# Hybrid Conformer/SSD block: sums of weight blocks by adding loads and another VectorE order at the hand-over to the feed forward

## The chip, the core and the metric

One core of a Trainium2 chip runs the whole block in one program. TensorE (PE in the profile) does the matmuls, VectorE (DVE) and ScalarE (ACT) the elementwise work, GpSimd (POOL) a few small operations and the loads that add to what lies in memory on the chip, SyncE (SP) issues most of the plain loads. The metric is the device time of one execution in microseconds (us). Before the change it is 1030.28 us, the median of three runs (1030.25 to 1030.38).

## What is computed

A block of a language model on 512 tokens of width 1024: a mixer with two branches (a gated convolution and a state space scan), then a gated feed forward. The mixer is unchanged here; what matters is its end and the feed forward behind it.

```python
h = rms_norm(x, mix_pre_g); proj = h @ w_in
...
mixed = (g_conv * conv_out + g_ssm * ssm_out) @ w_out
x = x + rms_norm(mixed, mix_post_g)
h = rms_norm(x, ffn_pre_g)
gt, up = jnp.split(h @ w_gate_up, 2, axis=-1)
f = (jax.nn.silu(gt) * up) @ w_down
x = x + rms_norm(f, ffn_post_g)
```

`FFN_HIDDEN` is 2816, so the gate and the up part have 22 tiles of 128 columns each, and `rms_norm(y, g)` is `y * rsqrt(mean(y*y) + 1e-6) * g`.

## The kernel before

**Arithmetic.** Every float32 operand of a matmul is split into a high and a low half of a shorter type, and a product takes three matmuls (`mm3`, L186 to L188: high by high, high by low, low by high). The high half is a cast by ScalarE, the low half the difference by VectorE (`halve`, L930 and L935). For the units listed in `ADD_LO`, ScalarE writes the negated high half instead (L932) and an adding load on GpSimd's queue adds the weight to it from memory (L933).

**The feed forward by Strassen-Winograd.** The product `h @ w_gate_up` is done in 22 pairs of tiles, the units `u = 0..21` (in pairs: the even units are gate parts, the odd ones up parts; pair `f = u // 2`), each with seven block products in place of eight. A unit has two weight blocks of 128 x 1024, each read as a left and a right half of 512 columns: (a11, a12) and (a21, a22). Weight sums of a unit are made by VectorE in `prep_s`: s1 = a21 + a22 (L956), s3 = a11 + a21 (L959, into a21's place), s2 = s1 + a11 (L960), s4 = s2 + a12 (L961). The activations' blocks b11, b21, b22 and their sums t1 to t4 are made in `transposed` once the four token tiles are there. TensorE multiplies a11 by b11, a12 by b21, s1 by t1, s2 by t2, s3 by t3, s4 by b22 and a22 by t4, 12 matmuls of 256 columns for each product. Products that belong together are added in one PSUM bank where that is possible, and by VectorE otherwise (`add`, L1107).

**The hand-over.** Token tile 3 is the last of the mixer. `tm_step` puts out its last product with the output weights (`tm_wo`; their last matmuls read the tiles named m1h and m1l in the pool `mp`). `residual(3)` then takes the mean square of each half (ScalarE, tile jk), the sum pm_a (VectorE, L873), the power -1/2 (GpSimd, rs_a, L874), the scaled sum with the old x (VectorE, xr, L1006), again mean square, pm_b, rs_b, and a diagonal matrix dg = identity times rs_b (VectorE, L1010). TensorE transposes xr by multiplying with dg (tile ptr, L1023). `transposed(3)` makes the tiles xg (L1030 on VectorE, L1035 on ScalarE) and from them t1 (L1061), t2 (L1062), t3 (L1068), t4 (L1070) and b22 with their halves. TensorE meanwhile runs the first products of units 0 to 2 (`first`), which need only the tokens of earlier tiles for the first part.

**Order.** Each engine runs its instructions in the order of its queue; a waiting instruction holds what stands behind it. The order is decided when the program is built, from the program's text, the tiles' dependences and a planner; `not_before(a, b)` keeps instruction a behind b. The list `hold` gives two instructions, for ScalarE and VectorE, behind which the halves of weights have to stay at that place. `start` (L1205) gives the order of the last products of the first four units: `v0 x0 v1 w0 y0`, then `x1 w1 z0 y1` and so on, where v is s1's product, x is s2's, w is s4's with b22, y is s3's and z is a22's with t4 - each letter a function (v1, x2, v2, x3, x4 in the code).

**Results of units.** Gate units write to tiles sg, up units to two slots each of f32, an array of 22 slots of 2 KB a partition. f32 is made (L1158) after `mix.close()`, so it takes space on the chip that the pool `mp` has given up; its first write has to wait for all that was there. For a unit, `begin` copies the first product out of PSUM (ScalarE, L1118) and adds the second (VectorE, L1107); `v1` copies s1's product from its own bank v (ScalarE, L1170), and the product with b22 later starts anew in that same bank (`v2`), so it waits for that copy.

**Loads.** `w_raw(n)` loads the n-th weight block (512 KB) on SP's queue into one of five buffers, in the order of `ORDER` (L148).

## Time and profile before

| | us |
|---|---|
| median of 3 runs | 1030.28 (1030.25 to 1030.38) |
| the profiled execution | 1036.17 |
| its span, first to last instruction | 1034.4 |
| TensorE busy | 1024.2 |
| VectorE busy | 814.3 |
| ScalarE busy | 609.0 |
| GpSimd busy | 96.4 |
| mean granted TensorE clock | 0.998 |

The profiled execution is longer than the runs that are only timed, so times of the trace are compared with the trace's own span, and times of runs with runs. Engines have the names given above; PEld is the loading of weights into TensorE's array. A timeline row has the start, the duration, the engine, the line of the kernel, the operation, output and inputs by the names of tiles, their size, and in brackets the idle time before it with what ended that. A tile's name stands there without its number: `xy` is a bank with two quarter results of a unit, `v` the bank of s1's product, `ptr` a transposed tile, `whi_g`/`wlo_g` and `chi_g`/`clo_g` the high and low halves of a weight block (two names for two places), `dhi`/`dlo` those of s1, `s` is s1, `raw` a weight block as loaded, `f` is f32. The hand-over lies between 690 and 745 us of the span.

### The profile page before, as it was taken

The page shows a single profiled execution, that of the slowest core. Times are in us where ns is not written, and L with a number is a line of the kernel's source. Part 1 is how long each engine was busy: PE and PEld are TensorE (multiplying, and loading weights), DVE is VectorE, ACT ScalarE, POOL GpSimd, SP SyncE. Part 2 cuts the span into 40 slices and gives each one's busy share as a digit, 9 for nine tenths or more (in the row PEclk, how much of TensorE's full clock was granted, in tenths as well). Part 3 has the DMA queues.
Part 4 walks back from the last instruction along what each step waited for, and adds up shares of the span by engine and source line. Part 5 has one row for each costly group of instructions (what it writes and reads, how often), then busy time and mean ns, then how long its engine had stood idle before and what let it go on. Part 6 is the DMA issues. An engine that isn't in the chain of part 4 may idle for free.

```text
span 1034.4 us, 15686 instructions
## 1 busy us (share of the span) xinstructions
PE 1024.2 (99%) x6089; PEld 890.9 (86%) x6089; DVE 814.3 (79%) x1184; ACT 609.0 (59%) x1032; POOL 96.4 (9%) x122
## 2 busy tenths in 40 slices
PE   9999999999999999999999999999999999999997
PEld 7898889888888888888888888889999999998885
DVE  7899976959594979398976455579997788799874
ACT  7655776575748464844532673366665565568552
POOL 0101101110111011101100000010000000001000
PEclk9999999999999999999999999999999999999999
DMA  8567634655546454644452223433565345469622
GB/s 298 156 164 213 165 81 140 184 157 148 135 131 163 124 157 128 163 122 122 110 133 84 82 85 99 183 105 121 167 184 157 105 143 146 123 197 278 214 82 82
DMA packets 42458, 150.82 MB, mean 146 GB/s; under 512 B 4880, under 2 KB 5904, under 8 KB 41360
## 3 DMA queue, kind: packets, MB, share of 16 engines
q1 hardware_dynamic: 30672, 104.66, 29.9%
q0 software_dynamic: 9504, 38.80, 19.0%
q10 hardware_dynamic: 2208, 6.36, 1.8%
q8 instruction: 48, 0.79, 0.3%
q14 instruction: 26, 0.21, 0.1%
HBM read 145.54 MB, written 4.26 MB: 145 GB/s over the span
## 4 chain that ended last, share of the span: by engine, by line
PE 93%; DVE 3%; ACT 2%; issue 1%; DMA 0%; POOL 0%; SPq 0%; ACTq 0%; POOLq 0%; DVEq 0%
PE xy L187 4%; PE xy L186 4%; PE xy L188 4%; PE pz L187 3%; PE pz L188 3%; PE pz L186 3%; PE pso L186 3%; PE pso L187 3%; PE pso L188 3%; PE px L188 3%; PE px L187 3%; PE px L186 3%; PE yv L187 2%; PE yv L188 2%; PE yv L186 2%; PE yd L636 2%
## 5 line engine op out<-in xcount | busy, mean ns | idle before, releaser
L152 ACT CAST whi<-raw 128x1024 fp32r<-128x1024 f32 (+2 forms) x116 | 115.0, 1003 | 157.3 <-PE pso L187 37.5
L444 DVE SCALAR_TENSOR_TENSOR a<-v,prm_t,a 128x511 f32<-128x511 f32 (+15 forms) x240 | 179.8, 752 | 16.1 <-ACT a L441 13.8
L158 DVE TENSOR_TENSOR wlo<-raw,whi 128x1024 fp32r<-128x1024 f32 (+2 forms) x76 | 85.8, 1134 | 42.8 <-ACT whi L152 42.1
L156 POOL DMA_DIRECT2D wlo<-in_w x40 | 35.7, 893 | 353.5 <-ACT wlo L155 120.9
L188 PE MATMUL pz<-whi,hlo 128*128 128x512 f32 (+2 forms) x160 | 56.3, 352 | 0.0
L187 PE MATMUL pz<-wlo,hhi 128*128 128x512 f32 (+2 forms) x160 | 56.1, 351 | 0.0
L186 PE MATMUL pz<-whi,hhi 128*128 128x512 f32 (+2 forms) x160 | 55.4, 353 | 0.0
L186 PE MATMUL px<-hhi,whi 128*128 128x512 f32 x128 | 50.2, 392 | 0.0
L186 PE MATMUL pso<-yh,whi 128*128 128x512 f32 x128 | 50.0, 393 | 0.0
L188 PE MATMUL px<-hhi,wlo 128*128 128x512 f32 x128 | 49.8, 389 | 0.0
L187 PE MATMUL px<-hlo,whi 128*128 128x512 f32 x128 | 49.8, 389 | 0.0
L187 PE MATMUL pso<-yl,whi 128*128 128x512 f32 x128 | 49.7, 390 | 0.0
L188 PE MATMUL pso<-yh,wlo 128*128 128x512 f32 x128 | 49.7, 389 | 0.0
L930 ACT CAST whi_g<-raw 128x1024 fp32r<-128x1024 f32 x40 | 41.3, 1053 | 13.7 <-PE yv L187 8.6
L528 DVE SCALAR_TENSOR_TENSOR x<-px,prm_t,x 128x511 f32<-128x511 f32 (+2 forms) x48 | 34.7, 741 | 13.8 <-ACT x L526 13.8
L935 DVE TENSOR_TENSOR wlo_g<-raw,whi_g 128x1024 fp32r<-128x1024 f32 x34 | 41.1, 1218 | 5.1 <-ACT whi_g L930 4.7
L155 ACT ACTIVATE wlo<-whi 128x1024 fp32r<-128x1024 f32 x40 | 42.2, 1055 | 0.3
L426 ACT ACTIVATE L<-L,nacs 128x128 f32<-128x128 f32 x128 | 38.8, 389 | 0.5 <-POOL L L419 0.4
L186 PEld LDWEIGHTS pz<-whi,hhi 128*128 128x128 f32 x160 | 30.2, 189 | 3.9
L187 PEld LDWEIGHTS pz<-wlo,hhi 128*128 128x128 f32 x160 | 30.2, 188 | 3.8
L188 PEld LDWEIGHTS pz<-whi,hlo 128*128 128x128 f32 x160 | 30.1, 188 | 3.7
L930 ACT CAST chi_g<-raw 128x1024 fp32r<-128x1024 f32 x24 | 24.8, 1050 | 11.4 <-PE yv L187 5.1
(656 smaller groups left out, 3344.8 us busy)
## 6 DMA issues: line engine op xcount, KB each, us to landing
raw<-in_w SPq DMA_DIRECT2D x186, 512.0 KB, 4.5
wlo<-in_w POOLq DMA_DIRECT2D x40, 512.0 KB, 6.8
L<-scr POOLq DMA_DIRECT2D x8, 1024.0 KB, 7.1
wlo_g<-in_w POOLq DMA_DIRECT2D x11, 512.0 KB, 7.1
clo_g<-in_w POOLq DMA_DIRECT2D x7, 512.0 KB, 5.3
xr<-in_x ACTq DMA_DIRECT2D x4, 512.0 KB, 4.7
x2d<-xr ACTq DMA_DIRECT2D x4, 512.0 KB, 2.9
xres<-x2d SPq DMA_DIRECT2D x4, 512.0 KB, 3.7
```

What stands on the lines that cost most here:

```text
L152: act.copy(hi[:, c], src[:, c])
L155: act.activation(lo[:, c], hi[:, c].bitcast(F32), AF.Copy, scale=-1.0)
L156: mark["lo"] = pool.dma_start(lo[:, c], w[n][:, c].bitcast(F32R), accum_op=ALU.add)
L158: mark["wlo"] = dve.tensor_tensor(out=lo[:, c], in0=src[:, c], in1=hi[:, c].bitcast(F32), op=ALU.subtract)
L186: mark["pe"] = pe.matmul(ps, lh, rh, start=start, stop=False, skip_group_check=more)
L187: pe.matmul(ps, lh, rl, start=False, stop=False, skip_group_check=more)
L188: mark["pe3"] = pe.matmul(ps, ll, rh, start=False, stop=stop, skip_group_check=more)
L426: act.activation(L[:, h, c, :], L[:, h, c, :], AF.Exp, bias=nacs[:, c, HG * g + h : HG * g + h + 1])
L444: return dve.scalar_tensor_tensor(out=va[j][:, d:], in0=vs[j][:, : T - d], scalar=col("dw_w", j * KC + KC - 1 - d), in1=va[j][:, d:], op0= ...
L528: dve.scalar_tensor_tensor(out=a[:, d:], in0=ps[:, : T - d], scalar=col("ssm_w", i * KS + KS - 1 - d), in1=a[:, d:], op0=ALU.mult, op1=ALU ...
L930: a_ = act.copy(hi, src)
L935: d_ = dve.tensor_tensor(out=lo, in0=src, in1=hi.bitcast(F32), op=ALU.subtract)
```

## The change

Nothing that is multiplied changes, and neither does TensorE's order of instructions.

- *Sums by loads.* For units 1 and 2, s1 is loaded as a21 (`load_s1`, a plain load on SP's queue) and a22 is added to it by an adding load on GpSimd's queue (`add_s1`); s3 is made by adding a11 to a21 in the loaded block in the same way (`add_s3`). s1 of unit 2 lies in the room of m1l, and the second blocks of units 1 and 2 (tile b12) in the room of m1h, so their loads are issued after the last `tm_wo` matmul that reads these. VectorE has L956 and L959 less for these two units.
- *Unit 4's low half* by ScalarE and an adding load (`ADD_LO`).
- *Order of VectorE around token tile 3.* `hold` is set after xr in place of after mg; in unit 0's halves the later part is held behind dg; unit 1's sum s2 is held in place of s1; the sum of unit 3 is held behind t4's low half. `add_s1` and `add_s3` are held behind the last power.
- *d1.* The first half of unit 1's result gets a tile of its own (d1, in the pool of sg) and `begin(1)` comes earlier. The second half takes its slot of f32 only at the copy in `v1`. The product with the gate is written to f32 by the last step (`f_out`), and the same function names the places of other units as before.

In the built order the instructions of VectorE are 5 fewer, ScalarE has one more, and GpSimd issues 5 more loads. On GpSimd's queue the add to s1 of unit 2 stands ahead of the power for rs_b of token tile 3; the adds to b12 stand behind it. On ScalarE's queue the copy of s1's product of unit 1 into f32 stands behind the two whi_g casts, the table load and the Silu of unit 0; in the kernel before it stood ahead of them.

```diff
--- before.py
+++ after.py
@@ -75,7 +75,7 @@
 EARLY_U = 4
 DMA_EVERY = 2
 DMA_FROM = 8
-ADD_LO = (2, 3) + tuple(range(7, FF // P, 2))
+ADD_LO = (2, 3, 4) + tuple(range(7, FF // P, 2))
 GU_AHEAD = 5
 MOV_AT = 192
 S_AHEAD = 5
@@ -136,12 +136,15 @@
 
 
     raws, split, more_raw = {}, {}, []
+    late = {}
     seq = {key: n for n, key in enumerate(ORDER)}
     GU = range(seq["gu", 0], seq["w1", 0])
 
     def w_raw(n):
-        if n < len(ORDER) and n not in raws:
-            if more_raw and n >= GU[0] and n % 7 < 2:
+        if n < len(ORDER) and n not in raws and late.get(n, True) is not None:
+            if n in late:
+                raws[n] = late[n]
+            elif more_raw and n >= GU[0] and n % 7 < 2:
                 raws[n] = more_raw[0].tile([P, 1024], F32, tag="raw2", bufs=2, name=f"raw{n}")
             else:
                 raws[n] = wp.tile([P, 1024], F32, tag="raw", bufs=RAW_BUFS, name=f"raw{n}")
@@ -871,7 +874,7 @@
         rs = sm.tile([P, 1], F32, tag="rs1", bufs=2, name=f"rs_{tag}")
         m = sm.tile([P, 1], F32, tag="pm1", bufs=2, name=f"pm_{tag}")
         mark["pm"] = dve.tensor_scalar(out=m, in0=ss[0], scalar1=ss[1], scalar2=RMS_EPS, op0=ALU.add, op1=ALU.add)
-        pool.tensor_tensor(out=rs, in0=m, in1=neg_half[:, :1], op=ALU.pow)
+        mark["pow"] = pool.tensor_tensor(out=rs, in0=m, in1=neg_half[:, :1], op=ALU.pow)
         return rs
 
     def scale_of(srcs, pool_, tag):
@@ -946,18 +949,41 @@
             again = w[seq[("gu", 2 * u)]] if u in ADD_LO else None
             halve(("a11", "a12"), u, g_raw(u, 0), room or pair_of_tiles(), again)
 
+    s1s = {}
+
+    def load_s1(u):
+
+        if u == 1:
+            s1s[u] = w2.tile([P, T], F32, tag="s1", bufs=2, name=f"s1_{u}")
+        else:
+            s1s[u] = mp.tile([P, T], F32, tag="m1l", name=f"s1_{u}")
+        nc.sync.dma_start(s1s[u], w[seq["gu", 2 * u + 1]][:, :T])
+
+    def add_s1(u):
+
+        return pool.dma_start(s1s[u], w[seq["gu", 2 * u + 1]][:, T:], accum_op=ALU.add)
+
+    def add_s3(u):
+
+        return pool.dma_start(g_raw(u, 1)[:, :T], w[seq["gu", 2 * u]][:, :T], accum_op=ALU.add)
+
     def prep_s(u):
 
         if u >= NF or (u, "s1") in forms:
             return
         ra, rb_ = g_raw(u, 0), g_raw(u, 1)
         (a11, a12), (a21, a22) = [(r[:, :T], r[:, T:]) for r in (ra, rb_)]
-        s1_ = w2.tile([P, T], F32, tag="s1", bufs=2, name=f"s1_{u}")
-        sum_ = dve.tensor_tensor(out=s1_, in0=a21, in1=a22, op=ALU.add)
+        if u in s1s:
+            s1_ = s1s[u]
+        else:
+            s1_ = w2.tile([P, T], F32, tag="s1", bufs=2, name=f"s1_{u}")
+            sum_ = dve.tensor_tensor(out=s1_, in0=a21, in1=a22, op=ALU.add)
+            if u == 3:
+                not_before(sum_, mark["t4"][1])
+            dve.tensor_tensor(out=a21, in0=a11, in1=a21, op=ALU.add)
+        sum_ = dve.tensor_tensor(out=a11, in0=s1_, in1=a11, op=ALU.add)
         if hold:
             not_before(sum_, hold[1])
-        dve.tensor_tensor(out=a21, in0=a11, in1=a21, op=ALU.add)
-        dve.tensor_tensor(out=a11, in0=s1_, in1=a11, op=ALU.add)
         dve.tensor_tensor(out=a12, in0=a11, in1=a12, op=ALU.add)
 
         def s1_halves():
@@ -967,6 +993,8 @@
             halve(("s2", "s4"), u, ra, pair_of_tiles())
             if u != 1:
                 s1_halves()
+            if u == 0:
+                hold[1] = mark["dg"]
             halve(("s3", "a22"), u, rb_, pair_of_tiles())
 
         if u == 1:
@@ -986,6 +1014,8 @@
             if k == 0 and mark.get("chain"):
                 not_before(m, last)
 
+    b12_raw = [seq["gu", 2 * u + 1] for u in (1, 2)]
+    late.update({n: None for n in b12_raw})
     xrs, xgs = {}, {}
 
     def residual(t, ps):
@@ -997,14 +1027,15 @@
         ss = []
         for n, c in enumerate(cols2):
             ss.append(mean_sq(ps[n], pbp, f"a{t}", n))
-            m = dve.tensor_tensor(out=mg[:, c], in0=ps[n], in1=gpost0[:, c], op=ALU.mult)
-        if t == 3:
-            hold += [mark["sq"], m]
+            dve.tensor_tensor(out=mg[:, c], in0=ps[n], in1=gpost0[:, c], op=ALU.mult)
+        first_sq = mark["sq"]
         rs = factor(ss, f"a{t}")
         ss = []
         for n, c in enumerate(cols2):
-            dve.scalar_tensor_tensor(out=xr[:, c], in0=mg[:, c], scalar=rs, in1=xr[:, c], op0=ALU.mult, op1=ALU.add)
+            m = dve.scalar_tensor_tensor(out=xr[:, c], in0=mg[:, c], scalar=rs, in1=xr[:, c], op0=ALU.mult, op1=ALU.add)
             ss.append(mean_sq(xr[:, c], pbp, f"b{t}", n))
+        if t == 3:
+            hold += [first_sq, m]
         rs = factor(ss, f"b{t}")
         dg = pbp.tile([P, P], F32, tag="dg", name=f"dg{t}")
         mark["dg"] = dve.tensor_scalar(out=dg, in0=ident, scalar1=rs, scalar2=None, op0=ALU.mult)
@@ -1094,6 +1125,10 @@
             sums()
         if (t, k) in ((3, 1), (3, 2)):
             prep_a(k + 1)
+        if (t, k) == (3, 2):
+            load_s1(1)
+        if (t, k) == (3, 6):
+            not_before(add_s1(1), mark["pow"])
         if (t, k) == (3, 4):
             halves = prep_s(0)
         if (t, k) == (3, 5):
@@ -1111,7 +1146,10 @@
     def begin(u):
 
         f, e = u // 2, u % 2
-        if e == 0:
+        if u == 1:
+            d1 = h2e.tile([P, T], F32, tag="d1", bufs=1, name="d1")
+            D_[u] = [d1, None]
+        elif e == 0:
             sg[f] = D_[u] = [h2e.tile([P, T], F32, tag=f"sg{i}", bufs=2, name=f"sg{f}_{i}") for i in range(2)]
         else:
             D_[u] = [f32[:, 2 * f + i, :] for i in range(2)]
@@ -1130,20 +1168,29 @@
         product(X[u], u, "a11", "b11", True)
         product(Y[u], u, "a12", "b21", u >= EARLY_U)
 
+    room = mp.tile([P, 2, 1024], F32, tag="m1h", name="b12")
+    for i, n in enumerate(b12_raw):
+        late[n] = room[:, i]
+        w_raw(n)
+    load_s1(2)
     halves()
-    hold[1] = mark["pm"]
     mark["chain"] = True
     for u in range(3):
         first(u)
         if u == 0:
+            hold[1] = mark["pm"]
             halves = prep_s(1)
+    for u in (1, 2):
+        not_before(add_s3(u), mark["pow"])
+    add_s1(2)
     sums, rest = transposed(3)
     pb.close()
     h2e = h2.enter_context(tc.tile_pool(name="h2e", bufs=2))
     more_raw.append(h2e)
+    sums()
     begin(0)
-    sums()
     rest()
+    begin(1)
     hold[:] = mark["t3"]
     halves()
     hold[:] = mark["t4"]
@@ -1157,6 +1204,9 @@
     fp = ctx.enter_context(tc.tile_pool(name="f", bufs=1, side="right"))
     f32 = fp.tile([P, NF, T], F32, name="f32")
 
+    def f_out(u, i):
+        return f32[:, u - 1 + i, :] if u % 2 else D_[u][i]
+
     def x2(u):
         if u not in D_:
             begin(u)
@@ -1167,17 +1217,19 @@
         if u < EARLY_U:
             V[u] = bank(f"v{u}")[:, :HB]
         product(V[u], u, "s1", "t1", True)
+        if u == 1:
+            D_[u][1] = f32[:, 1, :]
         act.copy((D_[u][1] if u in D_ else begin(u)[1])[:, c2], V[u])
 
     def x3(u):
         f, e = u // 2, u % 2
-        d = D_[u][1][:, c2]
+        d, to = D_[u][1][:, c2], f_out(u, 1)[:, c2]
         product(X[u], u, "s3", "t3", False)
         add(d, X[u])
         if e == 0:
             act.activation(d, d, AF.Silu, scale=-1.0)
         else:
-            gated_by(d, d, sg[f][1][:, c2])
+            gated_by(to, d, sg[f][1][:, c2])
 
     def v2(u):
         f, e = u // 2, u % 2
@@ -1187,7 +1239,7 @@
         if e == 0:
             act.activation(d, d, AF.Silu)
         else:
-            dve.tensor_tensor(out=d, in0=d, in1=sg[f][0], op=ALU.mult)
+            dve.tensor_tensor(out=f_out(u, 0), in0=d, in1=sg[f][0], op=ALU.mult)
 
     def x4(u):
         f, e = u // 2, u % 2
@@ -1196,7 +1248,7 @@
         if e == 0:
             act.activation(d, X[u], AF.Silu, scale=-1.0)
         else:
-            gated_by(d, X[u], sg[f][1][:, c1])
+            gated_by(f_out(u, 1)[:, c1], X[u], sg[f][1][:, c1])
 
     def gated_by(out_, src, by):
         dve.scalar_tensor_tensor(out=out_, in0=src, scalar=-1.0, in1=by, op0=ALU.mult, op1=ALU.mult)
```

## The prediction

> **What bounds the kernel now.** The page comes first: it names the engine that sets the time.

> ```profile
> span 1034.4 us, 15686 instructions
> PE 1024.2 (99%) x6089; PEld 890.9 (86%) x6089; DVE 814.3 (79%) x1184; ACT 609.0 (59%) x1032; POOL 96.4 (9%) x122
> ```

> TensorE (PE) is busy for 1024.2 of 1034.4 us. So a change that leaves the matmuls alone can win only the gaps between them, and costs whatever new gap it opens. Next comes TensorE's view of waits in the window of the hand-over (693 to 745 us), and the stretches there: time, PE busy, PEld, DVE, ACT, POOL, granted clock, DMA share, GB/s.

> ```profile
> PE xy L186 <- DVE f L1107: 0.8, 2, 0.4
> ...
> 700.00:712.00 12.00, 11.50 (x100) 11.13 (x99) 10.87 (x19) 6.99 (x17) 2.49 (x2) 1.00 0.42 139
> 712.00:730.00 18.00, 17.09 (x140) 16.35 (x141) 17.84 (x30) 12.34 (x23) 0.00 (x0) 1.00 0.35 116
> ```

> TensorE idles 0.50 us in the first stretch and 0.91 in the second, and in the second VectorE (DVE) is busy for 17.84 of 18.00: VectorE is what TensorE waits for. The gaps one by one, and the matmuls that the argument needs, from TensorE's timeline (start, duration, what it ran):

> ```profile
> 697.37 0.39 PE L187 MATMUL tm_wo<-wlo,m1h 128*128 128x512 f32 x1
> ...
> 706.23 0.28 PE L188 MATMUL xy<-b21h,wlo_g 128*128 128x256 f32 x1
> 706.59 2.02 PE L1023 MATMUL ptr<-dg,xr 128*128 128x128 f32 x16
> 711.88 0.38 PE L187 MATMUL v<-t1l,dhi 128*128 128x256 f32 x1 [0.42 <-DVE t1l L1041]
> 719.28 0.39 PE L186 MATMUL xy<-t2h,chi_g 128*128 128x256 f32 x1 [0.42 <-DVE f L1107]
> 719.74 0.28 PE L186 MATMUL xy<-t2h,chi_g 128*128 128x256 f32 x1
> 720.76 0.28 PE L186 MATMUL v<-b22h,chi_g 128*128 128x256 f32 x1
> 721.78 0.28 PE L186 MATMUL v<-b22h,chi_g 128*128 128x256 f32 x1
> 722.35 0.39 PE L186 MATMUL xy<-t4h,chi_g 128*128 128x256 f32 x1
> 728.89 0.38 PE L186 MATMUL xy<-t4h,chi_g 128*128 128x256 f32 x1 [0.42 <-DVE f L1107]
> 729.35 0.28 PE L186 MATMUL xy<-t4h,chi_g 128*128 128x256 f32 x1
> 735.00 0.28 PE L186 MATMUL xy<-t4h,whi_g 128*128 128x256 f32 x1
> 741.72 0.28 PE L186 MATMUL xy<-t4h,whi_g 128*128 128x256 f32 x1
> ```

> From 719.74 to 721.78 lie 18 matmuls, 0.1133 us each; from 729.35 to 735.00 48, 0.1177 each. A matmul is drawn with 0.28 though the next starts after 0.11, so 0.17 of each gap is hidden in the drawing, and the one after a wait comes 0.11 later than usual. A marked wait of 0.42 therefore costs 0.42 + 0.17 + 0.11 = 0.70; the gap ahead of 722.35 costs 0.23 (721.78 plus three matmuls is 722.12) + 0.11. The six larger gaps from 706.59 to 728.89 cannot hold more than the 1.41 of idle time plus 6 x 0.28 = 3.1 us. That is all that the change can win.

> **The change, part by part.** *1. Five VectorE instructions less.* For units 1 and 2 the sum a21 + a22 and the sum a11 + a21 become loads with adding loads on GpSimd's (POOL's) queue; unit 4's low half goes to ScalarE (ACT) and an adding load. VectorE's rows around the last token tile:

> ```profile
> 699.87 0.20 DVE L873 TENSOR_SCALAR pm_a<-ss_a,ss_a 128x1 f32<-128x1 f32 x1
> 700.20 1.22 DVE L935 TENSOR_TENSOR wlo_g<-raw,whi_g 128x1024 fp32r<-128x1024 f32 x1
> 701.89 1.41 DVE L1006 SCALAR_TENSOR_TENSOR xr<-mg,rs_a,xr 128x512 f32<-128x512 f32 x2 [0.46 <-POOL rs_a L874]
> ...
> 704.96 0.20 DVE L873 TENSOR_SCALAR pm_b<-ss_b,ss_b 128x1 f32<-128x1 f32 x1
> 705.08 0.68 DVE L956 TENSOR_TENSOR s<-raw 128x512 f32<-128x512 f32 x1
> 706.21 0.29 DVE L1010 TENSOR_SCALAR dg<-ident,rs_b 128x128 f32<-128x128 f32 x1 [0.44 <-POOL rs_b L874]
> ...
> 708.22 0.68 DVE L1030 TENSOR_TENSOR xg<-ptr,prm_t 128x512 f32<-128x512 f32 x1
> ...
> 710.20 0.69 DVE L1062 TENSOR_TENSOR t<-t,xg 128x512 f32<-128x512 f32 x1
> ...
> 738.05 0.67 DVE L935 TENSOR_TENSOR dlo<-s,dhi 128x512 fp32r<-128x512 f32 x1
> 738.65 1.20 DVE L935 TENSOR_TENSOR clo_g<-raw,chi_g 128x1024 fp32r<-128x1024 f32 x1
> 739.78 0.41 DVE L1107 TENSOR_TENSOR f<-xy,f 128x256 f32<-128x256 f32 x1
> 740.12 1.20 DVE L935 TENSOR_TENSOR clo_g<-raw,chi_g 128x1024 fp32r<-128x1024 f32 x1
> ```

> Start to start, VectorE takes 0.60 us for a half block (738.05 to 738.65), 1.13 for a whole one (to 739.78), 0.34 for a quarter (to 740.12). Four sums gone are 4 x 0.60, the low half 1.13: 3.5 us of VectorE in all.

> *2. The re-ordered scale.* In the built order xr now stands ahead of wlo_g. GpSimd's power for it:

> ```profile
> 691.99 0.56 POOL L874 TENSOR_TENSOR rs_b<-pm_b,neg_half 128x1 f32<-128x1 f32 x1 [0.45 <-DVE pm_b L873]
> 693.98 0.89 POOL L933 DMA_DIRECT2D wlo_g<-in_w  x1 [1.43 <-ACT wlo_g L932]
> 700.23 1.63 POOL L874 TENSOR_TENSOR rs_a<-pm_a,neg_half 128x1 f32<-128x1 f32 x1 [5.35 <-DVE pm_a L873]
> ...
> 705.31 0.86 POOL L874 TENSOR_TENSOR rs_b<-pm_b,neg_half 128x1 f32<-128x1 f32 x1 [3.45 <-DVE pm_b L873]
> ```

> Beside VectorE's wlo_g (700.20 to 701.42) the power took 1.63 and ended at 701.86, 0.44 after it; elsewhere 0.56. With VectorE now idle it ends at 700.23 + 0.56 = 700.8, xr starts there (1.1 us sooner), and xr x2 (1.2), wlo_g (1.13) and dlo (0.60) put pm_b at 703.8, done by 704.0 instead of 705.16.

> *3. A new wait on GpSimd's queue, ahead of the second power.* The built order puts the adding load for s1 of unit 2 before rs_b. It waits for s1's plain load, third on SP's queue behind two 512 KB loads into m1h's room, which the last tm_wo matmul frees at 697.37 + 0.39 = 697.8. The DMA views of two windows (655 to 657, then 688 to 706; size, median us from issue to landing):

> ```profile
> raw<-in_w SPq DMA_DIRECT2D x3, 512.0 KB, 5.6
> ```

> ```profile
> wlo_g<-in_w POOLq DMA_DIRECT2D x2, 512.0 KB, 7.6
> raw<-in_w SPq DMA_DIRECT2D x2, 512.0 KB, 3.6
> ```

> Bounds for that load: 3.6 as if alone, 701.4; 5.6 behind others, with 0.33 to issue each of two before it, 704.0; beside a wlo_g add as slow as 7.6, 706. I take 704.0, the row that is like it. Behind the waiting issue stands rs_b, behind that dg, the transposes and xg. So: issue 0.89 (704.9), rs_b 0.12 + 0.56 (705.6), dg to 705.9. TensorE asks at 706.34, so the 0.25 at 706.59 is won; a landing after 704.4 delays TensorE one for one. Then VectorE's clo_g (1.13) and two halves stand ahead of xg: 708.2, as before; t (L1062) starts at 709.6 instead of 710.20, since one sum between them is gone. If the load lands early the chain is up to 0.4 better (709.2), not more: rs_b then meets VectorE's next sum (703.9 to 704.6) and is held to 0.44 past its end, as rs_a was. [...]

> *4. A new wait on ScalarE's queue.* Unit 1's first half moves from f32 to a tile of its own, d1, so f32's first write becomes the copy of v1 into f32. f32 lies in the space of the closed pool that held m1h and m1l; its first write waits for all that lies there, now also the two b12 blocks and s1. In the built order that copy is behind whi_g x2, the table load and the Silu, and waits for VectorE's wlo_g of b12; before it stood ahead of them:

> ```profile
> 717.46 0.38 ACT L1170 COPY f<-v 128x256 f32<-128x256 f32 x1
> ...
> 721.35 1.28 ACT L1188 ACT_TABLE_LOAD   x1
> ...
> 723.18 1.99 ACT L930 CAST whi_g<-raw 128x1024 fp32r<-128x1024 f32 x2
> ```

> TensorE's second product into the same bank (v<-b22h, unit 1, at 720.76) cannot start until the copy has read it. The first whi_g waits for VectorE's last sum of unit 2: from t at 709.6, 11 halves, 3 quarters and 2 wholes later, 6.6 + 1.0 + 2.3 = 9.9, done at 719.7. Then ScalarE: 1.9 for the whi_g x2, 1.28 table, 0.55 Silu (the gap from the load's end, 722.63, to 723.18), 0.38 copy: 723.9. TensorE, which would have been at v<-b22h some 0.7 earlier than before, now stands for nearly 4 us: 723.9 against 720.76 is +3.1. Part comes back, as the waits at 722.35 and 728.89 vanish under it: 0.34 + 0.70 = 1.05 (smaller gaps some 0.2 more): +1.9 to +2.1 from here.

> *5. VectorE's order towards the add f<-xy (739.78).* Against the old order, 2 wholes and 3 halves more stand between t (L1062) and this add: 2 x 1.13 + 3 x 0.60 = 4.1 us; 47 instructions before, 52 now. VectorE ran without idle time there, so the add starts 4.1 later less the 0.6 that t is earlier, 739.78 + 3.5 = 743.3, about 743.4 with some 0.1 for dependent starts, and ends at 743.8. Unit 3's last product (741.72) needs it: 743.85, +2.1, and the 0.11 after a wait: **+2.2 us**. It masks step 4 rather than adding to it. I see nothing later that returns it: PE was full from 730 on.

> *6. Other edits at nothing.* Unit 4's ScalarE copy (about 1 us, as one whi_g) and the further adding loads are covered by ScalarE's idle time (12.34 busy of 18.00) and GpSimd's (0.00). The tightest add is b12 of unit 1: issued at 705.6, behind rs_b, it has until about 715.2, when ScalarE casts it (chi_g): 9.6 us, where twice its size took 7.6. Were it later than that, TensorE's waits would shift by the excess.

> **The sum** is made against the profiled execution: its time of 1036.17 (span 1034.4 and 1.8 around it) becomes 1038.4. The runs' median is 1030.28, 0.994 of that, so 2.2 stays 2.2: 1032.5. This measurement can tell about 0.2% from no change, 2.06 us: 1028.2 to 1032.34.

> **The rivals.** *A: a little less, within 0.2%.* The s1 load lands by 703.5 and t starts at 709.2: both chains are 0.4 earlier, +1.8, 1032.1. For it: 3.6 us for loads that go alone. Against: two loads stand before it, and wlo_g's add, issued at 693.98, is still on its way until 701.6.

> *B: more.* The loads share the DMA engines with that add and land at 705 or 706: rs_b, dg, transposes, xg and every sum after them move 1 or 2 us, +3.2 to +4.2, 1033.5 to 1034.5. Later raw loads that wait for a freed buffer may add 0.5. Against: the second landing needs 7.6 us for an SP load, 2 more than its row.

> *C: not slower.* TensorE's cadence goes from 0.1133 to 0.1177 near 723 us and the trace gives no cause (granted clock 1.00 in both). If a long pause ahead of it puts the slower cadence off, 10 us win 0.37 (0.0044 / 0.1177), and about 60 us decide: there the loss is paid, 1030.3; 100 us give 1028.8, and 150 faster, 1026.9. Against: after the wait at 728.89 the cadence is still 0.1177. Nothing in the rows has a pause of 4 us to judge by.

> *D: the change does not do what it says.* The wait on f32's first write does not bind, so step 4 falls and the gaps are won. Step 5 stands without it: VectorE alone keeps +2.2. Only if both fell would it be faster, 1030.3 - 3.1 = 1027.2 at best. Against: the waits and both orders stand in the built program.

> **How the numbers follow.** Forecast, +2.06 to +2.9: 0.42. B: 0.20. A: 0.27. C or D: 0.11, of which 0.09 are faster and 0.02 within. That makes slower 0.62, same 0.29, faster 0.09. The range leaves out C and D and the far end of B: from 1031.4 (steps 4 and 5 each shorter by 1 us than the rows say) to 1034.9 (a landing at 706 and some raw loads late).

> **What would show it.** Right: no gap ahead of the transposes and of v<-t1l; rs_a at 0.56; a wait of 3 to 4 us of TensorE at v<-b22h for ScalarE's copy, which starts behind the Silu near 723.5; no waits at xy<-t4h of units 0 and 1; VectorE's add f<-xy ending near 743.8 and TensorE's last product of unit 3 just after it, 2.1 later than before; from there both kernels in step to the end. Wrong: TensorE at v<-b22h near 720 (step 4 falls); the add before 742 (step 5 falls); rs_b after 706.2 (B); a cadence of 0.1133 after 730 (C).

## The result and the profile after

The changed kernel takes 1043.62 us (median of 4 runs, 1039.76 to 1045.62) against 1030.33 (1030.25 to 1030.39): ratio 1.0125, interval 1.0092 to 1.0157. The prediction said 1032.5; slower was right, the size was not. Executions of every kernel here, the one before included, fall into two groups some 6 us apart (before, in all its runs: 1029.6 to 1031.7 and 1035.9 to 1037.5), which in the 15 profiled ones go with TensorE's cadence between some 760 and 910 us, 0.1133 or 0.1177 us for 256 columns; where medians of the lower group alone are compared below, the text says "at 0.1133". The profiled executions of before and after are both at 0.1177 and can be compared: the 9.4 us between their spans are what has to be explained, as the 13.3 between the medians hold part of that gap too.

The page of the kernel after, its waits of TensorE (whole span), and the stretches of the hand-over (time, PE, PEld, DVE, ACT, POOL, granted clock, DMA share, GB/s):

```profile
span 1043.8 us, 15704 instructions
PE 1027.1 (98%) x6089; PEld 893.7 (86%) x6089; DVE 813.5 (78%) x1179; ACT 609.5 (58%) x1033; POOL 99.6 (10%) x127
```

```profile
PE v L189 <- ACT f L1222: 3.7, 1, 3.7
PE ptr L1054 <- issue: 3.2, 1, 3.2
```

```profile
700.00:712.00 12.00, 8.78 (x78) 8.62 (x77) 6.61 (x12) 4.70 (x10) 3.62 (x5) 1.00 0.88 262
712.00:730.00 18.00, 14.21 (x106) 13.81 (x106) 17.27 (x28) 12.30 (x24) 0.23 (x1) 0.88 0.44 109
730.00:760.00 30.00, 30.00 (x246) 30.00 (x246) 28.85 (x44) 18.91 (x31) 0.88 (x1) 0.96 0.55 173
```

The small waits of before (0.4 each) are gone, and two long stands have come: 3.2 us at the transposes and 3.7 us at v<-b22h of unit 1. The clock column is new too: 1.00 throughout before, now 0.88 and 0.96. TensorE's timeline, then GpSimd's, SP's and the DMA issue (697 to 715 us) that belong to the first stand:

```profile
707.35 0.28 PE L191 MATMUL xy<-b21h,wlo_g 128*128 128x256 f32 x1
710.85 2.53 PE L1054 MATMUL ptr<-dg,xr 128*128 128x128 f32 x16 [3.22 <-issue]
...
729.53 0.58 PE L189 MATMUL v<-b22h,chi_g 128*128 128x256 f32 x1 [3.68 <-ACT f L1222]
...
738.10 0.28 PE L189 MATMUL xy<-t4h,chi_g 128*128 128x256 f32 x1
```

```profile
701.34 0.56 POOL L877 TENSOR_TENSOR rs_a<-pm_a,neg_half 128x1 f32<-128x1 f32 x1 [5.37 <-DVE pm_a L876]
708.95 0.89 POOL L964 DMA_DIRECT2D s<-in_w  x1 [7.04 <-DMA s<-in_w]
709.56 0.86 POOL L877 TENSOR_TENSOR rs_b<-pm_b,neg_half 128x1 f32<-128x1 f32 x1
```

```profile
699.88 0.43 SPq L960 DMA_DIRECT2D s<-in_w  x1
```

```profile
s<-in_w SPq DMA_DIRECT2D x1, 256.0 KB, 8.4
```

TensorE is done with what it has at 707.35 + 0.11. dg needs rs_b; rs_b stands on GpSimd's queue behind the adding load to s1 of unit 2, and that waits for the plain load, which was issued at 699.88 and landed 8.4 us after, at 708.27; the adding load starts 0.68 later, at 708.95. (The page's "issue" names no releaser; GpSimd's bracket names the load.) The second stand, on ScalarE and VectorE:

```profile
724.57 0.68 DVE L987 TENSOR_TENSOR raw<-raw 128x512 f32<-128x512 f32 x1
...
727.57 1.22 DVE L938 TENSOR_TENSOR wlo_g<-b,whi_g 128x1024 fp32r<-128x1024 f32 x1
```

```profile
725.28 1.05 ACT L933 CAST whi_g<-raw 128x1024 fp32r<-128x1024 f32 x1 [2.58 <-DVE raw L987]
726.24 1.04 ACT L933 CAST whi_g<-b 128x1024 fp32r<-128x1024 f32 x1
727.29 1.28 ACT L1240 ACT_TABLE_LOAD   x1
728.59 0.63 ACT L1240 ACTIVATE sg<-sg 128x512 f32<-128x512 f32 x1
729.12 0.35 ACT L1222 COPY f<-v 128x256 f32<-128x256 f32 x1
```

VectorE's last sum of unit 2 ends at 725.25, then two casts, the table load, the Silu and only then the copy of v1, done at 729.47; TensorE goes on at 729.53. ScalarE has no idle time ahead of the copy, so its turn on the queue sets the time; but the last row that reads b12's room, VectorE's wlo_g of b, ends at 728.79, so a free ScalarE could have been at most some 0.3 us earlier. Behind each stand the clock falls; stretches of half a microsecond around the first:

```profile
712.00:712.50 0.50, 0.50 (x5) 0.50 (x5) 0.50 (x2) 0.00 (x0) 0.23 (x1) 0.69 0.89 156
...
715.00:715.50 0.50, 0.50 (x4) 0.50 (x4) 0.50 (x2) 0.50 (x4) 0.00 (x0) 0.50 0.77 168
715.50:716.00 0.50, 0.50 (x6) 0.50 (x5) 0.50 (x2) 0.50 (x2) 0.00 (x0) 0.90 0.71 188
```

The clock is 0.50 in the six stretches from 712.5 to 715.5; with the two edges (0.69, 0.90) that is 0.5 x (0.31 + 6 x 0.5 + 0.10) = 1.71 us of full clock lost, or 3.41 us at one half. The second fall, behind 729, sums to the same 1.71.

**Where the time went.** TensorE's last matmul ahead of the transposes starts at 706.23 before and 707.35 after (1.12 late already, gathered in parts that the change leaves alone; the second trace of the kernel before, r5, is 0.90 late there), the first xy<-t4h of unit 1 at 728.89 and 738.10. So 9.21 - 1.12 = 8.1 us were lost between, and the spans differ by 9.4. The stands, start to start beyond the cadence, are 3.39 (710.85 - 707.35 - 0.11) and 3.85 (3.68 shown + 0.17 hidden); with two falls of the clock, 3.42, that is 10.7. The gaps of before, at most 3.1, are swallowed: 7.6 at least; the other 0.5 is not broken down.

### The profile page after: what moved, and what is told of

The parts are those of the page before. It is cut to its first block, busy times and chain, and to the rows that moved or that the text cites. A ratio compares the mean times of both kernels' runs of the same rounds, so it can differ in the third digit from the quotient of the medians.

```text
span 1043.8 us, 15704 instructions
## 1 busy us (share of the span) xinstructions
PE 1027.1 (98%) x6089; PEld 893.7 (86%) x6089; DVE 813.5 (78%) x1179; ACT 609.5 (58%) x1033; POOL 99.6 (10%) x127
## 4 chain that ended last, share of the span: by engine, by line
PE 90%; DVE 4%; ACT 3%; issue 1%; DMA 0%; POOL 0%; SPq 0%; ACTq 0%; DVEq 0%; POOLq 0%
PE xy L190 4%; PE xy L191 4%; PE xy L189 4%; PE pso L189 3%; PE pso L190 3%; PE pso L191 3%; PE pz L190 3%; PE pz L191 2%; PE yv L191 2%; PE px L191 2%; PE px L189 2%; PE yv L189 2%; PE yv L190 2%; PE px L190 2%; PE pz L189 2%; PE pgs L191 1%
## 5 line engine op out<-in xcount | busy, mean ns | idle before, releaser
L933 ACT CAST whi_g<-raw 128x1024 fp32r<-128x1024 f32 x39 | 40.2, 1053 | 19.1 <-PE yv L190 9.9
L938 DVE TENSOR_TENSOR wlo_g<-raw,whi_g 128x1024 fp32r<-128x1024 f32 x32 | 38.7, 1221 | 5.5 <-ACT whi_g L933 5.2
L933 ACT CAST chi_g<-raw 128x1024 fp32r<-128x1024 f32 x23 | 23.9, 1051 | 12.1 <-PE yv L190 5.4
## 6 DMA issues: line engine op xcount, KB each, us to landing
raw<-in_w SPq DMA_DIRECT2D x184, 512.0 KB, 4.4
wlo<-in_w POOLq DMA_DIRECT2D x40, 512.0 KB, 6.4
wlo_g<-in_w POOLq DMA_DIRECT2D x12, 512.0 KB, 7.7
clo_g<-in_w POOLq DMA_DIRECT2D x7, 512.0 KB, 5.6
xr<-in_x ACTq DMA_DIRECT2D x4, 512.0 KB, 4.5
x2d<-xr ACTq DMA_DIRECT2D x4, 512.0 KB, 2.9
xres<-x2d SPq DMA_DIRECT2D x4, 512.0 KB, 4.3
```

Source lines behind the costliest of these rows:

```text
L933: a_ = act.copy(hi, src)
L938: d_ = dve.tensor_tensor(out=lo, in0=src, in1=hi.bitcast(F32), op=ALU.subtract)
```

## The experiments

Theory L: a late plain load makes the first stand, through the adding load ahead of the power on GpSimd's queue, and f32's first write makes the second; each stand costs a fall of the clock besides. Its rivals: a disturbed execution, another releaser of the transposes, the planner's order alone, and VectorE's longer order (step 5). Theory G, on the clock alone, is told where it is tried (r6). The table has all runs: ratio to the runs of before with its interval, the difference of medians at 0.1133, TensorE's long stands and the falls of the clock in the profiled execution.

| run | ratio | at 0.1133, us | stands, us | falls, us lost |
|---|---|---|---|---|
| r1 changed kernel again | 1.0100 (1.0065 to 1.0135) | +8.6 | 3.0, 3.7 | 1.7, 1.7 |
| r5 before again | 0.9994 (0.9964 to 1.0025) | -0.2 | none over 0.5 | none |
| r2 power first | 1.0054 (1.0030 to 1.0078) | +5.1 | 3.9 | 1.7 |
| r3 own tile | 1.0106 (1.0066 to 1.0146) | +9.7 (two runs) | 3.0, 1.9 | 1.7, 1.7 |
| r4 both | 1.0050 (1.0022 to 1.0079) | +3.1 | 2.0, 1.4 | 1.7 |
| r6 before, 3 powers | 0.9997 (0.9966 to 1.0028) | +0.8 | 1.0 | none |
| r7 before, 5 powers | 1.0014 (0.9987 to 1.0042) | +2.6 | 2.2 | none |
| r11 before, 7 powers | 1.0068 (1.0050 to 1.0087) | +5.5 | 3.9 | 3.4 |
| r8 s1 loaded first | 1.0093 (1.0061 to 1.0125) | +10.4 | 4.7, 3.9 | 1.7, 1.7 |
| r13 no add ahead | 1.0072 (1.0050 to 1.0094) | +5.9 | 3.9 | 1.7 |
| r10 order alone | 1.0105 (1.0081 to 1.0130) | +6.3 (one run) | 1.1, 3.9 | 1.7 |
| r9 both, copies first | 1.0054 (1.0037 to 1.0071) | +4.7 | 4.4 | 3.4 |
| r12 and low half back | 0.9971 (0.9947 to 0.9994) | -1.5 | none over 0.7 | none |

**r1, the changed kernel again** (no edit).

> The changed kernel again, for its spread. Theory L (the plain load of s1 for unit 2 lands late, its adding load holds rs_b on GpSimd's queue, TensorE stands about 3 us at the transposes; ScalarE's copy of v1 makes a second stand of about 4 us; after each the granted clock is near 0.5 for about 3 us): the two stands are there again, 3 to 4 us each, and the time is 8 to 15 us above before. Rival R (a disturbed execution): the stands are gone or the clock stays 1.00, and the time is near +2 us.

Both stands and both falls are there again (3.0 and 3.7 us). Its profiled execution was one at 0.1133 (1039.15 us), so the cadence is not the kernel's; a second profile of the kernel before (r5) was at 0.1133 too:

> The kernel before, again, for a second trace of it. If TensorE's cadence of 0.1177 us from 723 us on belongs to the kernel, it is there again; if it belongs to the single execution, this trace can have 0.1133 up to the last stage and then a span some 6 us shorter.

Its span is 1028.9 us against 1034.4, ratio 0.9994 (0.9964 to 1.0025). The same program, the same waits of 0.4 to 0.5 us, 5.5 us less. So it was its cadence, and not the profiling, that made the first profiled execution of the kernel before (1036.17) longer than its timed runs.

**r2, the power first.**

```diff
-    add_s1(2)
+    not_before(add_s1(2), mark["pow"])
```

> Only change against the changed kernel: the adding load to s1 of unit 2 is held behind rs_b's power on GpSimd's queue. Theory L: no stand at the transposes, rs_b starts within 0.3 us of pm_b's end, granted clock 1.00 until about 722, and the stand at v<-b22h of unit 1 stays, 3 to 4 us; the time lies 2 us above before plus what the clock costs after one stand, some 4 to 6 us above before. Rival: if the transposes wait for something else (the x2d store, xr), the stand of 3.2 us stays.

GpSimd's queue and TensorE's waits (from 600 us on):

```profile
705.08 0.86 POOL L877 TENSOR_TENSOR rs_b<-pm_b,neg_half 128x1 f32<-128x1 f32 x1 [3.45 <-DVE pm_b L876]
706.38 1.83 POOL L968 DMA_DIRECT2D b<-in_w  x2 [0.44 <-issue]
708.25 0.87 POOL L964 DMA_DIRECT2D s<-in_w  x1
```

```profile
PE v L189 <- ACT f L1222: 3.9, 1, 3.9
PE xy L189 <- ACT sg L1214: 0.4, 1, 0.4
PE xy L189 <- DVE f L1142: 0.3, 1, 0.3
```

rs_b no longer waits for a load, the first stand is gone with its fall, and the time (+5.1) is in the range expected; s1 still lands 8.0 us after its issue, now harmlessly. The last row is step 5 of the prediction, 0.3 us of it, as the stand of 3.9 hides the rest.

**r3, the copy to a tile of its own, and r4, both edits.**

```diff
-            D_[u] = [d1, None]
+            D_[u] = [d1, h2e.tile([P, HB], F32, tag="d1b", bufs=1, name="d1b")]
...
-        if u == 1:
-            D_[u][1] = f32[:, 1, :]
-        act.copy((D_[u][1] if u in D_ else begin(u)[1])[:, c2], V[u])
+        act.copy(D_[u][1] if u == 1 else (D_[u][1] if u in D_ else begin(u)[1])[:, c2], V[u])
```

> Only change against the changed kernel: the copy of s1's product of unit 1 goes to a tile of its own, not to f32, so it does not wait for what lay in f32's space. Theory L: the stand at the transposes stays (about 3 us, clock near 0.5 for some 3 us), the stand at v<-b22h is gone; 4 to 7 us above before. Rival (the copy waits for ScalarE's order, not for f32's space): the stand at v<-b22h stays.

> Both edits together. Theory L: no stand over 1 us between 700 and 745, granted clock 1.00 there, and a time within 2 us of before, likely 0 to 0.5 us below it. Rival (VectorE's longer order alone, step 5 of the prediction): unit 3's last product still waits for VectorE and the time is about 2 us above before.

In both the stand at v<-b22h is gone: with a room of its own the copy stands ahead of the casts again, so its late place came from f32's space. But the times expected were wrong, r3's (+9.7, not 4 to 7) as well as r4's: another stand came in its place, with a fall of its own (1.9 us in r3, 2.0 in r4). r4's waits of TensorE and its ScalarE timeline:

```profile
PE xy L189 <- ACT d L1214: 2.0, 1, 2.0
PE xy L189 <- DVE f L1142: 1.4, 1, 1.4
```

```profile
717.71 0.37 ACT L1220 COPY d1b<-v 128x256 f32<-128x256 f32 x1
720.53 1.05 ACT L933 CAST whi_g<-raw 128x1024 fp32r<-128x1024 f32 x1 [2.45 <-DVE raw L987]
721.49 1.05 ACT L933 CAST whi_g<-b 128x1024 fp32r<-128x1024 f32 x1
722.55 1.28 ACT L1238 ACT_TABLE_LOAD   x1
...
725.20 0.36 ACT L1214 COPY d<-xy 128x256 f32<-128x256 f32 x1
```

The next copy of unit 1 (s2's product) also stands behind the casts and the table load, where the kernel before had it ahead (720.96 against the load's 721.35). And VectorE's late add of step 5 now shows, 1.4 us.

**r6, r7, r11, a stand by itself.** The kernel before computes rs_b of token tile 3 several times over; the rest of the program's text stays.

```diff
-        pool.tensor_tensor(out=rs, in0=m, in1=neg_half[:, :1], op=ALU.pow)
+        for _ in range(3 if tag == "b3" else 1): pool.tensor_tensor(out=rs, in0=m, in1=neg_half[:, :1], op=ALU.pow)
```

> The kernel before with the power of rs_b of token tile 3 computed three times in place of once (two more GpSimd instructions ahead of dg, every other order the same). Price of a stand by itself: TensorE stands about 1.5 us at the transposes. Theory G (a stand longer than some 1.6 to 1.9 us lowers the granted clock to 0.5 for about 3 us, a shorter one does not): clock stays 1.00, time about 1 us above before. Rival (any stand over 1 us lowers it): clock near 0.5 after the transposes.

> The same with five powers: TensorE stands about 2.8 us at the transposes. Theory G: the granted clock is 0.5 for about 3.3 us after it, which costs about 1.7 us more, part of which is taken from the waits behind; time 2.5 to 4.5 us above before. Rival (the low clock comes from the loads or from VectorE's order in the changed kernel, not from the stand): clock 1.00, time 2 to 2.5 us above.

> The kernel before with seven powers in place of one for rs_b: TensorE stands about 3.4 us at the transposes, as long as in the changed kernel. Theory G: the granted clock is 0.5 for about 3.3 us behind it, 4.0 to 5.5 us above before. Rival (the low clock comes from something else in the changed kernel): clock 1.00 as after the stand of 2.2 us, 3 to 3.6 us above.

Three, five and seven powers take 2.10, 3.33 and 4.68 us on GpSimd, and the stands are 1.0, 2.2 and 3.9. The same stretch of r7 and then of r11, behind the stand:

```profile
709.50:713.00 3.50, 2.89 (x25) 2.92 (x26) 3.28 (x7) 0.83 (x4) 0.18 (x1) 1.00 0.00 0
```

```profile
709.50:713.00 3.50, 1.72 (x8) 1.75 (x9) 2.09 (x4) 0.00 (x0) 1.20 (x3) 0.57 0.00 0
713.00:716.50 3.50, 3.50 (x18) 3.50 (x18) 1.65 (x3) 1.43 (x6) 0.00 (x0) 0.50 0.00 0
```

The stand makes the fall: no load and no ScalarE copy differs in r11, and the one other change of order, VectorE's sum L959 ahead of dg, ends at 707.36, long before dg at 710.89. The length of the stand alone does not decide: 2.2 us left the clock at 1.00 here, 1.9 us (r3) and 2.0 (r4) brought it down, all of 2.96 and more did. So theory G as it stood is wrong: in r7's trace the expected fall did not come, and that its time (+2.6) lies in the expected range, at the lower edge, is luck. r11 lost 3.4 us at the clock, 0.50 for 6.8 us, twice as long as most. What decides is in the last section.

**r8, s1 loaded first.**

```diff
+    load_s1(2)
     room = mp.tile([P, 2, 1024], F32, tag="m1h", name="b12")
...
         w_raw(n)
-    load_s1(2)
```

> Only change against the changed kernel: the plain load of s1 of unit 2 is issued ahead of the two b12 loads, not behind them. Theory L with the shared bandwidth as the cause of the late landing: s1 lands 1.5 to 3.5 us earlier (5 to 7 us after its issue in place of 8.4), the stand at the transposes is under 2 us and the low clock there is gone; the stand at v<-b22h stays; 4.5 to 7 us above before, near the kernel with the power first. Rival (the load waits for something else than the loads ahead of it): it lands 8 us after its issue again and the time stays 9 us above before.

s1 lands 6.3 us after its issue instead of 8.4, as expected, but the stand grew to 4.7 and the time to +10.4, neither as expected: the planner moved the adding load ahead of the first power too.

```profile
705.44 0.86 POOL L964 DMA_DIRECT2D s<-in_w  x1 [10.18 <-DMA s<-in_w]
706.01 0.88 POOL L877 TENSOR_TENSOR rs_a<-pm_a,neg_half 128x1 f32<-128x1 f32 x1
710.35 0.85 POOL L877 TENSOR_TENSOR rs_b<-pm_b,neg_half 128x1 f32<-128x1 f32 x1 [3.45 <-DVE pm_b L876]
```

The two loads ahead of it are worth 2.1 us of the landing, no more.

**r13, no adding load ahead.**

```diff
-ADD_LO = (2, 3, 4) + tuple(range(7, FF // P, 2))
+ADD_LO = (2, 4) + tuple(range(7, FF // P, 2))
```

> Only change against the changed kernel: unit 3's low half is made by VectorE at token tile 2, not by an adding load, so the adding load of 512 KB that is issued near 694 is gone and the plain loads behind it (b12 twice, s1 of unit 2) share the DMA engines with less. Theory L with that adding load as the cause of the late landing: s1 lands 4.5 to 6.5 us after its issue, not 8 to 8.4; the stand at the transposes is under 1.5 us, without a low clock behind it; the stand at v<-b22h stays; 4.5 to 7 us above before. Rival (the plain loads and the other transfers make it late by themselves): 7.5 us or more again, the stand is 2.5 us or longer and the time 8 to 10 us above before.

```profile
s<-in_w SPq DMA_DIRECT2D x1, 256.0 KB, 5.3
```

```profile
705.79 0.89 POOL L964 DMA_DIRECT2D s<-in_w  x1 [3.89 <-DVE pm_b L876]
```

With the same place on SP's queue, s1 lands after 5.3 us, at 705.14. The adding load still starts 0.65 us behind that landing (the bracket names pm_b, which ended in between, at 705.22), but this is early enough: the transposes start only 0.25 us behind what TensorE had. The time, +5.9, is as expected. So the one adding load of 512 KB, under way from 695.1 to 705.4 in the changed kernel, made the landing 3 us later, and the first stand with it.

**r10, the order alone.** Taken out: the adding loads of units 1 and 2, s1's loads, the room for b12, and 4 in `ADD_LO`.

> The changed kernel with its new order on VectorE and its tile d1, but without the adding loads and their rooms: VectorE makes all sums of units 1 and 2 and unit 4's low half. Theory L: no stand at the transposes and none at v<-b22h for the copy of v1, which stands ahead of the table load again, as nothing new lies in f32's space. VectorE has 5 instructions (3.5 us) more, so TensorE waits for it later: a wait of 3 to 4 us for a low half of unit 2 near 729; 3 to 6 us above before. Rival (the copy is late for the planner's order, not for f32's space): the stand at v<-b22h stays.

No wait for a copy into f32: it stands ahead of the table load again, as nothing new lies in f32's space, and the planner's order alone is not the cause. TensorE stands 3.9 us for VectorE, which has 5 instructions more. Expected were 3 to 4 us near 729 for a low half of unit 2; it is at 730.90, at a product of unit 2, and the releaser named is an add (sg) that stands behind two low halves (wlo_g) on VectorE. The time, +6.3, is a little above the 3 to 6 expected:

```profile
PE xy L189 <- DVE sg L1137: 3.9, 1, 3.9
```

**r9, both copies of unit 1 ahead, and r12, unit 4's low half back on VectorE** (r12 is r9 with `ADD_LO = (2, 3) + ...` as before).

```diff
-        a_ = act.copy(hi, src)
+        a_ = mark[names[0], u] = act.copy(hi, src)
...
-        act.copy(D_[u][0][:, c2], X[u])
+        c_ = act.copy(D_[u][0][:, c2], X[u])
+        if u == 1:
+            not_before(mark["s2", 2], c_)
+            not_before(mark["silu"], c_)
...
-            act.activation(d, d, AF.Silu)
+            mark["silu"] = act.activation(d, d, AF.Silu)
```

> The kernel with both edits (power first, own tile), and ScalarE's copy of s2's product of unit 1 held ahead of the whi_g cast of unit 2 and of unit 0's Silu, which puts both copies of unit 1 ahead of the table load as in the kernel before. Theory L with the order on ScalarE's queue as what is left: no stand over 1 us between 700 and 745, granted clock 1.00 there, 0.3 to 1.7 us below before. Rival (VectorE's longer order, step 5 of the prediction): a wait of 1 to 2 us for VectorE near 745 stays and the time is 0 to 2 us above before.

> The last version (power first, own tile, both copies of unit 1 ahead of the table load) with unit 4's low half made by VectorE again, as in the kernel before, not by an adding load. Theory: the adding load of unit 4, issued at 731.8 and landing 10 us later, made the only long stand of that version; without it no stand over 1 us between 700 and 760, clock 1.00, and 1 to 1.7 us below before (of the gaps' 3.1 us, less new waits of some 1.2 us for ScalarE and VectorE). Rival (VectorE's 1.13 us for the low half come back as a wait behind 739): within 0.5 us of before.

r9's ScalarE stand is gone, but the time (+4.7) was expected below before: TensorE, now earlier, waits for unit 4's low half:

```profile
PE xy L191 <- DMA wlo_g<-in_w: 4.4, 1, 4.4
```

In r12 what is left is two waits, and the clock stays at 1.00:

```profile
PE xy L189 <- DVE d1b L1142: 0.7, 1, 0.7
PE xy L189 <- ACT sg L1214: 0.4, 1, 0.4
```

r12 is ahead of both kernels: ratio 0.9971 (0.9947 to 0.9994) to before, and 1.5 us less at 0.1133, inside the expected 1 to 1.7; its trace gains 1.2 us on that of before between 690 and 745.

## Why the prediction was wrong, point by point

- *What bounds the kernel, and the most to win (3.1 us):* right as far as tried. r12 wins 1.2 to 1.5 of it. That the change is slower came out through steps 3 and 4, not through step 5, by which the sum went.
- *Step 2, the scale:* right. rs_a took 0.56 instead of 1.63; pm_b starts at 705.01, which less the 1.12 is 703.9, where 703.8 stood.
- *Step 3 is the one that failed.* The wait, its place on GpSimd's queue and everything behind it were named; the term that was mis-sized is the landing of s1's load. The prediction took 5.6 us, the row of three loads queued back to back; r13 measured 5.3 for just that, and 8.0 to 8.4 with wlo_g's adding load under way. Its outer bound, 706, was a landing after 7.6 and still short of 708.3 - 1.1 = 707.2. That is 2.8 later than the 704.4 from which it would "delay TensorE one for one"; another 0.6 comes from the steps behind it, as landing to transposes took 2.58 (708.27 to 710.85) and not 1.94 (704.4 to 706.34). So the 0.25 us won became a stand of 3.39. The rows of the prediction held the sign of it: rival A's text said that the add was on its way until 701.6.
- *A term was missing:* what a stand costs beyond its length. Step 4 forecast one of nearly 4 us and let TensorE go on at full clock behind it. Each of the two stands cost 1.71 us more. In r2, with step 4's stand alone, step 4's +1.9 to +2.1 and this term make 3.6 to 3.8; its trace loses 3.7 on that of before from 690 to 730 us. The medians at 0.1133 say +5.1, and 1.4 of that stay open.
- *Step 4, f32's first write:* right in mechanism and size. ScalarE's 4.1 us from the last sum of unit 2 to the end of the copy were 4.2 (725.25 to 729.47); the stand was 3.85 here and 4.07 in r2, start to start. r3 and r10 show the cause.
- *Step 5, VectorE's order:* right as a mechanism, but not what set the end. With TensorE 8 us late it hides; it is 0.3 in r2 and 1.4 in r4. "It masks step 4 rather than adding" held only while step 4 was priced without the clock.
- *Step 6, the rest at nothing:* true in the changed kernel, where TensorE is late; in r9, where it is not, unit 4's adding load is a stand of 4.4 us.
- *The rivals.* B was the right one, with its far end too near and its price without the clock. A and D did not happen; the wait on f32 binds. C fell: the cadence goes with the single execution (r5, r1), with or without a stand.

## What to carry to other kernels

On GpSimd's queue an adding load waited for its plain load, and rs_b stood behind it: the landing at 708.27, the adding load at 708.95, rs_b at 709.56. Put such a load behind what the critical chain needs (r2: +5.1 us, where r1 has +8.6), and price the plain load with the adding loads that are under way then (8.4 us from issue to landing, against 5.3 in r13, without the one issued at 695.10), not by plain rows. A stand of TensorE cost its length here and, if it was long enough, clock besides: none under 1.9 us did, every one of 2.96 us or more did, at 1.7 or 3.4 us, and between these it depended on where it lay (last section). Count both before trading several short waits for one long one. f32, in space taken over from a closed pool, had its first writer wait for what lay there: stands of 3.7 to 3.9 us, gone in r3 with a tile of its own. Such a writer should not be one that TensorE waits for.

## What the hardware showed that was not expected

| run, its stand | slot, us | its clock | TensorE busy in it, us | clock of the next slot |
|---|---|---|---|---|
| r4, 2.0 | 722.66 to 726.07 | 1.00 | 1.39 | 0.50 |
| r3, 1.9 | 727.97 to 731.38 | 1.00 | 1.52 | 0.50 |
| r7, 2.2 | 708.49 to 711.90 | 1.00 | 1.79 | 1.00 |
| after, 3.2 | 708.77 to 712.19 | 1.00 | 1.34 | 0.50 |
| r11, 3.9 | 706.60 to 710.02 | 1.00 | 0.78 | 0.50 |
| r11, going on | 710.02 to 713.43 | 0.50 | 2.15 | 0.50 |
| r8, 4.7 | 707.66 to 711.07 | 1.00 | 0.00 | 0.50 |
| r8, going on | 711.07 to 714.49 | 0.50 | 2.86 | 1.00 |

Over all slots of the 15 traces, one at 1.00 with 1.39 us or less of TensorE was always followed by 0.50 and one with 1.68 or more never; between them lie two, r3's 1.52 (a fall) and a 1.51 near the end of r7 (none). A slot at 0.50 was followed by another one with 2.15 (r11) and 2.24 (r9), and by 1.00 with 2.86 or more. So r7's 2.2 us were spread over two slots, with 2.79 and 1.79 left in them, while r3's 1.9 fell into one. As an estimate from these rows, a stand among otherwise full slots would cost clock when it leaves TensorE about 1.5 us or less of the 3.41 in one of them: one under 1.9 us (3.41 less 1.5) would not, one of 3.8 us or more, twice that, always would, and between the two it would depend on where the slots lie, which differs from one execution to the next (the first rise is at 5.63 in the trace after, at 5.86 in that before). r9's five runs at 0.1133 go with that: the shortest took 1033.44 us at a mean granted clock of 0.998, the longest 1036.76 at 0.995.

*Adding loads and the DMA engines.* In the changed kernel, with adding loads under way, the DMA engines are all busy (1.06, 1.03) and move little (239, 312 GB/s); later, with plain loads, they move more (1.02, 410; stretches, last two columns):

```profile
697.00:701.00 4.00, 3.93 (x25) 3.30 (x24) 2.46 (x5) 3.97 (x11) 0.00 (x0) 1.00 1.06 239
701.00:705.00 4.00, 4.00 (x38) 4.00 (x37) 3.25 (x6) 3.70 (x8) 0.56 (x1) 1.00 1.03 312
705.00:708.50 3.50, 2.63 (x24) 2.43 (x22) 0.82 (x3) 0.00 (x0) 0.00 (x0) 1.00 1.02 410
```

239 against 410 GB/s at nearly the same share of busy time. The view of packets by queue, from 697 to 715 us, agrees: the 1.55 MB of GpSimd's queue, all adding loads, took 50.6% of the 16 engines' time, the 1.92 MB of SP's plain loads 27.2%, so an adding load took 2.3 times as much for each MB. Whether that is the adding or the kind of queue, no run here separates.

*The two cadences* of one program, 0.1133 and 0.1177 us for 256 columns at a granted clock of 1.00, have no cause in any row here and stay open.
